# Attention rows of a one-core transformer layer: order of score blocks, output tail and products changed

## The chip, the core and the metric

The kernel runs on one core of one Trainium2 chip. A core has a matrix engine (TensorE, PE in the profile, with its weight loads as PEld), a vector engine (VectorE, DVE), a scalar engine for activation functions and copies (ScalarE, ACT), a general engine (GpSimd, POOL), and a queue engine that here only issues DMAs (SyncE, SP). Each engine works through its own instructions in order, and engines wait for each other through semaphores. Matrix results go to PSUM, which this stage divides into eight banks of 512 fp32 numbers in each of 128 partitions. The metric is the device time of one execution in microseconds (us).

## The reference

One layer of a hybrid backbone for two groups of tokens: 256 context tokens (the prompt) and 2048 latent tokens. Around the part that changes there are a projection, a Fourier mixing, an output projection and an MLP; they stay as they are. What changes is differential attention: for each of four heads there are two query/key halves, two softmaxes, and a difference of the two that is multiplied by the values.

```
s = jnp.einsum('bqhmd,bkhmd->bhmqk', qblk, k).astype(jnp.float32) * scale
p = jax.nn.softmax(s, axis=-1)
a = p[:, :, 0] - lam * p[:, :, 1]
return jnp.einsum('bhqk,bkhe->bqhe', a.astype(v.dtype), v)
```

Latent queries attend to 512 cached keys and to all 2048 latent keys, 2560 in all; prompt queries attend to the 256 prompt keys. Behind the attention each head's output is RMS-normalised.

## The kernel before

Before the attention stage, the kernel has written queries, keys and values to DRAM, most of them split into a high and a low part, so that fp32 products are made of three faster ones (`mm3`, L85 to L88).

**Groups and rows.** The stage runs over 4 heads and, in each, over 8 groups of 256 latent queries. A group is worked in four *rows*, one for each half j of its queries (128 each) and each softmax m: (j, m) = (0,0), (0,1), (1,0), (1,1). So there are 128 rows. In a row PE makes the five score blocks of the next row's softmax (`fill`, L918: 128 queries by 512 keys, two products each), VectorE takes the maximum of each block (`rowmax`, L923) and joins the five (`comb`, L926), and ScalarE makes the exponentials, with their sums, out of the five blocks that the row before had filled (`exp`, L942). When a half's two softmaxes are there, `combine` joins them: short VectorE work on the sums (L946, L947), then on GpSimd a scaling and an addition for the first 1024 keys and the same for the other 1536 (L964, L965).

**Products.** Six rows behind a group's start its products begin. The joined weights are transposed on PE in blocks of 2 x 128 keys for both halves (`tr`, L974, four transposes), ScalarE copies each transposed block out of PSUM (`ah`, L980), VectorE makes its low part (`al`, L985), and a row later PE multiplies by the values (`mul`). A group has ten such blocks, spread over four rows as 2, 3, 2 and 3. Two of the ten (key blocks 4 and 14, `FULL`) have no low part and are multiplied in plain fp32 (L998). The rows that transpose three blocks multiply two, and the rows that transpose two blocks multiply three, one of them in fp32.

**Output tail.** Five rows after its first transposes a group's output is finished. `o1` copies it out of PSUM (ScalarE, L1004), `o2` transposes it back (PE, L1008), `o3` copies that (VectorE, L1012), `o4` squares it with sums (ScalarE, L1018), `o5` makes the inverse root (VectorE L1021, then GpSimd L83), and `o6` scales it on GpSimd (L1027) and stores it with two DMAs (SyncE, L1028). All of that stands in the row in which the next group's first two blocks are multiplied; only the scaling spills into the row after it.

**Order.** The order of the work on each engine is written out by hand: `add(t, function, ...)` puts a step at a nominal time, in units `u` of a fifth of a row, and all steps are issued in the order of these times. The nominal times set only the order; the engines run when their waits are over. Prompt attention (`Prompt`) is put into a few rows of each head in the same way.

**PSUM.** Five banks (tag "S") hold score blocks, two (tag "pt") transposed blocks, one (tag "po") a group's output. With five score blocks a row and five banks, a block can be filled once the same block of the row before has been read by its exponential. A group allocates its own tile in the output bank with its first product:

```
if self.po is None:
    self.po = pS.tile([P, 512], F32, tag="po", name=f"po{self.nm}")
```

The first 256 columns take the sum of the products, the other 256 the transposed output.

Of the kernel before, what the change touches and what calls it, by code (L numbers as in the profile page):

```python
# [10 lines left out]
F32 = mybir.dt.float32  # L11
# [7 lines left out]
P = 128  # L19
# [21 lines left out]
def body(tc, a, out):  # L41
    nc = tc.nc
    ctx = ExitStack()
    with ctx:
# [40 lines left out]
        def mm3(ps, lh, ll, rh, rl, first, last):  # L85
            nc.tensor.matmul(ps, lh, rh, start=first, stop=False)  # L86
            nc.tensor.matmul(ps, lh, rl, start=False, stop=False)  # L87
            nc.tensor.matmul(ps, ll, rh, start=False, stop=last)  # L88
# [555 lines left out]
        with ExitStack() as c2:  # L644
# [106 lines left out]
            with tc.manual_schedule():  # L751
# [30 lines left out]
                A = [None] * 4  # L782
# [58 lines left out]
        with ExitStack() as c3_:  # L841
# [5 lines left out]
            ap = c3_.enter_context(tc.tile_pool(name="a_p", bufs=5, reuse_waits="tile"))  # L847
            kp = c3_.enter_context(tc.tile_pool(name="a_kp", bufs=1, reuse_waits="tile"))
            pS = c3_.enter_context(tc.tile_pool(name="a_ps", bufs=1, space=PSUM, reuse_waits="tile"))
            PCUT = 1024  # L850

            class Head:
# [28 lines left out]
            class Group:  # L881
                def __init__(self, hd, g):
                    self.hd, self.g, self.nm = hd, g, f"{hd.nm}_{g}"
                    self.S, self.mx, self.sm, self.p0, self.p1, self.tot = {}, {}, {}, {}, {}, {}
                    self.pt, self.A = {}, {}
                    self.po = None
                    self.nmul = 0
                    self.edge = 20 * g - 1 if hd.h == hd.s == 0 and g < 2 else None
                    self.last = hd.h == H - 1 and g == NS // 256 - 1

                    self.vcomb = 5 if self.last else 5 if hd.h == hd.s == g == 0 else 0
# [95 lines left out]

                def mul(self, kb):
                    if self.po is None:
                        self.po = pS.tile([P, 512], F32, tag="po", name=f"po{self.nm}")  # L990
                    A = self.A.pop(kb)
                    for t in range(2):
                        c = slice(t * 256, t * 256 + 256)
                        first = self.nmul == 0
                        self.nmul += 1
                        last = self.nmul == self.hd.nkt
                        if len(A) == 1:
                            nc.tensor.matmul(self.po[:, 0:256], self.hd.vf[kb][:, t, :], A[0][:, c], start=first, stop=last)  # L998
                        else:
                            mm3(self.po[:, 0:256], self.hd.V[:, kb + t, 0, :], self.hd.V[:, kb + t, 1, :], A[0][:, c], A[1][:, c], first, last)  # L1000

                def o1(self):
                    self.oT = at.tile([P, 256], F32, tag="oT", name=f"oT{self.nm}")
# [81 lines left out]
            def add(t, fn, *args):  # L1085
                ev.append((t, len(ev), fn, args))

            T = TSTEP
            u = T / 5.0
# [11 lines left out]
            for h in range(H):  # L1101
# [15 lines left out]
                for g in range(hd.ng):  # L1117
                    gr = Group(hd, g)
                    add(base - 2 * T + 0.6 * u if base else -3.03 * T, gr.qload)
                    for st in range(4):  # L1120
                        j, m = divmod(st, 2)
                        t0 = base + st * T
                        for b in range(hd.nbk):
                            add(t0 - T + (0.76 + 0.66 * b) * u, gr.fill, j, m, b)
                            add(t0 - T + (1.26 + 0.66 * b) * u, gr.rowmax, j, m, b)
                            add(t0 + 0.66 * b * u, gr.exp, j, m, b)
                        add(t0 - 0.45 * u, gr.comb, j, m)
                        if m:
                            add(t0 + 5.9 * u, gr.combine, j)
                    kbs = list(range(0, hd.nkt, 2))  # L1130
                    for q in range(4):
                        w = base + (AVS + q) * T
                        if q % 2 == 0:
                            order = [kbs.pop(0) for _ in range(2)]
                            tr_t, ah_t, al_t = [0.9, 2.2], [3.3, 3.8], [4.6, 5.2]
                        else:
                            order = [kbs.pop(0) for _ in range(3)]
                            tr_t, ah_t, al_t = [0.9, 2.2, 3.86], [3.3, 3.8, 4.4], [None, 4.6, 5.2]
                        for n, kb in enumerate(order):
                            add(w + tr_t[n] * u, gr.tr, kb)  # L1140
                            add(w + ah_t[n] * u, gr.ah, kb)
                            if al_t[n]:
                                add(w + al_t[n] * u, gr.al, kb)
                            add(w + T + (3.9 + 0.01 * n) * u, gr.mul, kb)
                    w = base + (AVS + 5) * T + 1.0 * u
                    for t, fn in ((0, gr.o1), (0.4, gr.o2), (0.75, gr.o3), (2.32, gr.o4), (3.557, gr.o5), (4.0, gr.o6)):
                        if gr.last and t > 2:
                            LASTO.append(fn)
                        else:
                            add(w + t * u, fn)  # L1150
                    base += 4 * T
# [754 lines left out]
```

## Time and profile before

| | |
|---|---|
| Median of 3 runs | 2971.24 us (2971.06 to 2977.52) |
| Profiled execution | 2976.96 us, span 2975.1 us |
| Instructions | 43755 |
| PE, PEld busy | 2910.2, 2518.0 us |
| DVE, ACT, POOL busy | 2016.3, 1568.3, 1023.9 us |
| Score products (L918), first to last | 571.3 to 1295.9 us of the span |
| Mean granted TensorE clock | 0.993 |

The span runs from the first to the last instruction of the profiled execution. "Busy" adds up the time in which an engine has an instruction running; PE's is an upper bound of its work, since matrix products are pipelined. In the timeline, a row gives the start and the length of a run of like instructions, the engine, the line of the kernel, the operation, output and inputs by the program's names, shapes and the count; brackets at the end give the idle time before it and what ended it. In the list of waits stand the engine, what it was about to write, whom it waited for, and the total, the count and the longest of these waits.

### The profile page before, as it was taken

The numbers are of one execution on the slowest core, as the hardware profiler recorded it, in microseconds if no ns is written. First come the engines' busy times: TensorE is split into PE (matmuls) and PEld (weight loads), VectorE is DVE, ScalarE is ACT, GpSimd is POOL, SyncE is SP. The second block draws the span as 40 slices with busy tenths as digits, with TensorE's granted clock in tenths as the row PEclk, the third lists the DMA queues.
The fourth block names the chain that finished last, engine by engine and source line by source line (L and its number), as shares of the span: only waits on it lengthen the run. The fifth ranks groups of instructions, "written<-read, shape, count | busy, mean of one in ns | idle before, by whom it ended". The sixth has DMA issues, their size and how long they took to land.

```text
span 2975.1 us, 43755 instructions
## 1 busy us (share of the span) xinstructions
PE 2910.2 (98%) x15417; PEld 2518.0 (85%) x15417; DVE 2016.3 (68%) x3379; ACT 1568.3 (53%) x3540; POOL 1023.9 (34%) x839
## 2 busy tenths in 40 slices
PE   8999999989999999999999999999999999999999
PEld 4888887768888888888889999999999888888887
DVE  6666775678888888875458778777776344344554
ACT  4333322678888888864346556556555322232221
POOL 1111112169898989952222333333332000000000
PEclk9999999989999999999999999999999999999999
DMA  7777878512131211215686677676666454445563
GB/s 274 202 195 198 232 197 250 195 52 84 35 110 37 91 53 34 95 50 157 202 252 213 217 240 225 220 237 214 222 199 229 145 170 163 138 145 173 195 216 107
DMA packets 394414, 495.58 MB, mean 167 GB/s; under 512 B 26403, under 2 KB 307056, under 8 KB 391122
## 3 DMA queue, kind: packets, MB, share of 16 engines
q1 hardware_dynamic: 386560, 477.63, 50.5%
q0 software_dynamic: 2992, 7.28, 0.8%
q10 hardware_dynamic: 4642, 7.88, 0.8%
q8 instruction: 122, 2.00, 0.3%
q14 instruction: 98, 0.80, 0.1%
HBM read 315.20 MB, written 179.57 MB: 166 GB/s over the span
## 4 chain that ended last, share of the span: by engine, by line
PE 84%; ACT 8%; DVE 4%; DMA 2%; issue 1%; POOL 0%; SPq 0%; ACTq 0%; DVEq 0%; POOLq 0%
PE Ss L918 8%; PE ps L86 8%; PE ps L87 8%; PE ps L88 8%; PE pj L86 4%; PE pj L88 4%; PE pj L87 4%; PE pts L974 4%; ACT P1s L942 3%; PE po L88 2%; PE po L86 2%; PE po L87 2%; PE pA L1532 2%; PE pA L1534 2%; PE pA L1533 2%; PE pC L1534 2%
## 5 line engine op out<-in xcount | busy, mean ns | idle before, releaser
L923 DVE TENSOR_REDUCE mxs<-Ss 128x1 f32<-128x512 f32 x640 | 419.4, 687 | 86.8 <-PE Ss L918 77.9
L1227 DVE TENSOR_TENSOR sl<-sr,sh 128x768 fp32r<-128x768 f32 x168 | 161.8, 964 | 339.8 <-ACT sh L1226 339.3
L965 POOL TENSOR_TENSOR P0s<-P0s,P1s 128x1024 f32<-128x1024 f32 x124 | 365.7, 2949 | 10.4
L1226 ACT CAST sh<-sr 128x768 fp32r<-128x768 f32 x168 | 140.2, 835 | 424.9 <-PE ps L87 424.9
L942 ACT ACTIVATE P1s<-Ss,mxs 128x512 f32<-128x512 f32 x320 | 217.2, 694 | 69.3 <-DVE mxs L926 69.3
L1574 POOL TENSOR_TENSOR gs<-g,g 128x384 f32<-128x384 f32 x48 | 70.3, 1464 | 483.7 <-ACT g L1544 376.7
L86 PE MATMUL pj<-wh,hh 128*128 128x512 f32 x576 | 229.8, 399 | 0.7 <-ACT fo L374 0.7
L87 PE MATMUL ps<-tlT,sh 128*128 128x512 f32 x585 | 229.3, 392 | 0.0
L86 PE MATMUL ps<-thT,sh 128*128 128x512 f32 x585 | 229.2, 392 | 0.0
L87 PE MATMUL pj<-wl,hh 128*128 128x512 f32 x576 | 227.7, 395 | 0.7 <-DVE wl L496 0.7
L88 PE MATMUL ps<-thT,sl 128*128 128x512 f32 x585 | 227.7, 389 | 0.0
L88 PE MATMUL pj<-wh,hl 128*128 128x512 f32 x576 | 226.7, 394 | 0.0
L942 ACT ACTIVATE P0s<-Ss,mxs 128x512 f32<-128x512 f32 x320 | 215.8, 696 | 7.8 <-DVE mxs L926 7.7
L918 PE MATMUL Ss<-KS1s,Qs 128*128 128x512 f32 x640 | 199.9, 426 | 13.6 <-ACT P0s L942 11.1
L918 PE MATMUL Ss<-KS0s,Qs 128*128 128x512 f32 x640 | 198.7, 423 | 10.5 <-ACT P1s L942 9.4
L974 PEld LDWEIGHTS pts<-ident,P0s 128*128 128x128 f32 x1280 | 158.0, 141 | 51.7 <-ACT ahs L980 5.7
L974 PE MATMUL pts<-ident,P0s 128*128 128x128 f32 x1280 | 193.0, 274 | 6.3 <-DVE alp L1071 4.1
L1543 ACT ACTIVATE g<-uz 128x384 f32<-128x384 f32 x144 | 75.9, 527 | 207.1 <-DVE uz L1566 180.6
L964 POOL TENSOR_SCALAR P1s<-P1s,tots 128x1024 f32<-128x1024 f32 x124 | 166.7, 1344 | 5.6
L985 DVE TENSOR_TENSOR als<-pts,ahs 128x512 fp32r<-128x512 f32 x256 | 163.9, 681 | 5.3 <-ACT ahs L980 5.3
L86 PE MATMUL ps<-ophT,sh 128*128 128x512 f32 x423 | 165.9, 392 | 1.1 <-DVE uz L1566 1.1
L88 PE MATMUL ps<-ophT,sl 128*128 128x512 f32 x423 | 165.7, 392 | 0.0
(613 smaller groups left out, 8216.1 us busy)
## 6 DMA issues: line engine op xcount, KB each, us to landing
sr<-sd SPq DMA_DIRECT2D x84, 768.0 KB, 4.4
a<-in_w SPq DMA_DIRECT2D x184, 256.0 KB, 3.8
sd<-gs SPq DMA_DIRECT2D x192, 192.0 KB, 1.9
sd<-g SPq DMA_DIRECT2D x144, 192.0 KB, 4.1
wm<-in_w_mod SPq DMA_DIRECT2D x32, 512.0 KB, 5.3
Qs<-qd SPq DMA_DIRECT2D x32, 512.0 KB, 3.7
b<-in_w SPq DMA_DIRECT2D x64, 256.0 KB, 5.2
b<-tsum SPq DMA_DIRECT2D x64, 256.0 KB, 4.6
```

Of the source, the lines that this page charges most:

```text
L86: nc.tensor.matmul(ps, lh, rh, start=first, stop=False)
L87: nc.tensor.matmul(ps, lh, rl, start=False, stop=False)
L88: nc.tensor.matmul(ps, ll, rh, start=False, stop=last)
L918: nc.tensor.matmul(S[:, :w], self.Q[:, x, m, j * P:j * P + P], self.hd.KS[m][:, b * 512:b * 512 + w], start=(x == 0), stop=(x == 1))
L923: nc.vector.tensor_reduce(self.mx[j][:, m, b:b + 1], self.S[j, m, b], axis=AX.X, op=ALU.max)
L942: nc.scalar.activation(dst, S, AF.Exp, bias=self.mx[j][:, m, 6:7], accum_out=self.sm[j][:, m, b:b + 1])
L964: nc.gpsimd.tensor_scalar(p, p, tot[:, 3:4], 0.0, op0=ALU.mult, op1=ALU.add)
L965: nc.gpsimd.tensor_add(d, d, p)
L974: nc.tensor.transpose(pt[:, c:c + P], self.p0[j][:, (kb + t) * P:(kb + t + 1) * P], ident)
L985: nc.vector.tensor_sub(t, self.pt[kb], f32(self.A[kb][0]))
L1226: nc.scalar.copy(hi, src)
L1227: nc.vector.tensor_sub(lo, src, f32(hi))
```

## The change

Five things in the attention stage, all in the order or the placing of work:

- The first transposed block of a row moves from behind score block 0 to behind score block 1, and the second from behind score block 2 to behind score block 3. The third stays behind score block 4.
- One PSUM tile `PO` serves all groups' output, instead of a tile for each group in the same bank.
- `o2` moves behind score block 1 of its row, and `o3` from between the first maxima of that row to behind its joined maximum and the subtractions, ahead of the next row's first maximum.
- `o4`, `o5` and `o6` move on by about a row: the squares go behind the next row's block copies, the inverse root and the scaling follow later in that row and the one after. The very last group keeps its own place for these three, and `o3` of it stays early.
- For key block 14, half of the first of its two fp32 products (the 128 queries of the first half) is taken a row earlier by `mul_part`; `mul` then does the other half of it, and the second product whole.

```diff
+            PO = pS.tile([P, 512], F32, tag="po", name="po")
...
-                    self.po = None
+                    self.po, self.half = None, []
...
-                        self.po = pS.tile([P, 512], F32, tag="po", name=f"po{self.nm}")
+                        self.po = PO
...
-                            nc.tensor.matmul(self.po[:, 0:256], self.hd.vf[kb][:, t, :], A[0][:, c], start=first, stop=last)
+                            x = P if kb in self.half and not t else 0
+                            nc.tensor.matmul(self.po[:, x:256], self.hd.vf[kb][:, t, :], A[0][:, t * 256 + x:t * 256 + 256], start=first, stop=last)
...
+                def mul_part(self, kb):
+
+                    self.half.append(kb)
+                    nc.tensor.matmul(self.po[:, 0:P], self.hd.vf[kb][:, 0, :], self.A[kb][0][:, 0:P], start=False, stop=False)
...
-                            tr_t, ah_t, al_t = [0.9, 2.2], [3.3, 3.8], [4.6, 5.2]
+                            tr_t, ah_t, al_t = [1.5, 2.8], [3.3, 3.8], [4.6, 5.2]
...
-                            tr_t, ah_t, al_t = [0.9, 2.2, 3.86], [3.3, 3.8, 4.4], [None, 4.6, 5.2]
+                            tr_t, ah_t, al_t = [1.5, 2.8, 3.86], [3.3, 3.8, 4.4], [None, 4.6, 5.2]
...
+                            if q == 3 and not n:
+                                add(w + 3.95 * u, gr.mul_part, kb)
...
-                    for t, fn in ((0, gr.o1), (0.4, gr.o2), (0.75, gr.o3), (2.32, gr.o4), (3.557, gr.o5), (4.0, gr.o6)):
-                        if gr.last and t > 2:
+                    for t, fn in ((0, gr.o1), (0.75, gr.o2), (0.95 if gr.last else 4.25, gr.o3), (8.5, gr.o4), (9.2, gr.o5), (9.6, gr.o6)):
+                        if gr.last and t > 5:
```

## The prediction

> **What bounds the kernel now.** I read the page first, then the stretches of time, the waits, and the timeline of one undisturbed group in the attention stage. All times are in microseconds.
>
> ```profile
> span 2975.1 us, 43755 instructions
> ...
> PE 2910.2 (98%) x15417; PEld 2518.0 (85%) x15417; DVE 2016.3 (68%) x3379; ACT 1568.3 (53%) x3540; POOL 1023.9 (34%) x839
> ```
>
> ```profile
> 650.00:1300.00 650.00, 635.90 (x4021) 538.51 (x4019) 564.11 (x1110) 573.41 (x1623) 582.79 (x469) 1.00 0.19 66
> ```
>
> The page's second line: TensorE works 98% of the span. The columns of the window are the length, then the busy time of PE, PEld, DVE, ACT and POOL, the granted clock, and DMA. In the 650 us that hold nearly the whole attention stage PE is busy 635.90, so PE's idle time there is 14.1; but each start after a wait also costs PE more than its idle time, as the rows below show. The four other columns are all at 83 to 90%: nothing has much room.
>
> ```profile
> DVE mxs L923 <- PE Ss L918: 77.9, 219, 2.4
> ...
> ACT P1s L942 <- DVE mxs L926: 69.3, 64, 5.2
> ...
> PEld Ss L918 <- ACT P0s L942: 31.9, 76, 2.5
> ```
>
> The three waits form a ring: maxima wait for scores, exponentials (exp) for the joined maximum, scores for an exp to empty their bank (five banks, five blocks a row). The rows of one group, on PE:
>
> ```profile
> 929.44 0.72 PE L918 MATMUL Ss<-KS1s,Qs 128*128 128x512 f32 x2
> ...
> 934.99 0.62 PE L918 MATMUL Ss<-KS0s,Qs 128*128 128x512 f32 x2
> ...
> 938.43 0.60 PE L974 MATMUL pts<-ident,P0s 128*128 128x128 f32 x4
> ...
> 940.68 0.73 PE L918 MATMUL Ss<-KS1s,Qs 128*128 128x512 f32 x2 [0.28 <-ACT P0s L942]
> ...
> 941.25 0.60 PE L974 MATMUL pts<-ident,P0s 128*128 128x128 f32 x4
> ...
> 943.98 1.02 PE L998 MATMUL pos<-ahs,vf4s 128*128 128x256 f32 x4
> ...
> 946.26 0.62 PE L918 MATMUL Ss<-KS0s,Qs 128*128 128x512 f32 x2
> ...
> 946.72 0.60 PE L974 MATMUL pts<-ident,P0s 128*128 128x128 f32 x4
> ...
> 949.45 0.60 PE L974 MATMUL pts<-ident,P0s 128*128 128x128 f32 x4
> ...
> 949.80 0.36 PE L86 MATMUL pos<-ahs,Vs 128*128 128x256 f32 x1
> ...
> 950.95 0.28 PE L86 MATMUL pos<-ahs,Vs 128*128 128x256 f32 x1
> ...
> 951.53 0.50 PE L918 MATMUL Ss<-KS1s,Qs 128*128 128x512 f32 x1
> ```
>
> A group of 256 queries takes four rows of work, each starting with score block 0 (L918): 929.44, 934.99, 940.68, 946.26, and the next group at 951.53. I call them R14 (ends with the fp32 products of block 14), RO (holds the old group's output tail), R4 (fp32 products of block 4) and RB. Lengths: 5.55, 5.69, 5.58, 5.27, together 22.09; 32 groups make 707 of the span. A score block costs 0.46 after products (946.26 to 946.72) and 0.57 when it had to wait (940.68 to 941.25). Four transposes take 0.35 (949.45 to 949.80); 946.72 to 949.45 is two such sets and two pairs of score blocks, so a pair takes 1.01, 0.505 for one in flow. RB's twelve products come in threes, 0.38 apart (949.80 to 950.95); the last three end at about 951.30, and PE then waits 0.23.
>
> ```profile
> 934.05 0.69 ACT L942 ACTIVATE P1s<-Ss,mxs 128x512 f32<-128x512 f32 x1 [1.01 <-DVE mxs L926]
> ...
> 938.11 0.36 ACT L1018 ACTIVATE osqs<-os 128x128 f32<-128x128 f32 x1
> ...
> 938.90 1.05 ACT L980 CAST ahs<-pts 128x512 fp32r<-128x512 f32 x2
> ...
> 939.84 0.70 ACT L942 ACTIVATE P0s<-Ss,mxs 128x512 f32<-128x512 f32 x1
> ...
> 945.29 0.69 ACT L942 ACTIVATE P1s<-Ss,mxs 128x512 f32<-128x512 f32 x1 [1.01 <-DVE mxs L926]
> ...
> 950.14 0.59 ACT L980 CAST ahs<-pts 128x512 fp32r<-128x512 f32 x1 [0.43 <-PE pts L974]
> ...
> 950.70 0.69 ACT L942 ACTIVATE P0s<-Ss,mxs 128x512 f32<-128x512 f32 x1
> ...
> 951.38 0.68 ACT L942 ACTIVATE P0s<-Ss,mxs 128x512 f32<-128x512 f32 x1
> ```
>
> ```profile
> 931.11 2.65 DVE L923 TENSOR_REDUCE mxs<-Ss 128x1 f32<-128x512 f32 x4 [0.21 <-PE Ss L918]
> ...
> 933.79 0.16 DVE L926 TENSOR_REDUCE mxs<-mxs 128x1 f32<-128x5 f32 x1
> ...
> 936.45 0.42 DVE L1012 COPY os<-pos 128x256 f32<-128x256 f32 x1
> ...
> 939.49 0.16 DVE L926 TENSOR_REDUCE mxs<-mxs 128x1 f32<-128x5 f32 x1
> ...
> 939.64 1.28 DVE L985 TENSOR_TENSOR als<-pts,ahs 128x512 fp32r<-128x512 f32 x2
> ...
> 946.92 0.69 DVE L923 TENSOR_REDUCE mxs<-Ss 128x1 f32<-128x512 f32 x1 [0.53 <-PE Ss L918]
> ...
> 950.51 0.16 DVE L926 TENSOR_REDUCE mxs<-mxs 128x1 f32<-128x5 f32 x1
> ```
>
> RO and RB end by the same ring: third transposed block, its copy (L980), exp 0, next score block. In RB: 949.45, 950.14, 950.70, 951.53, that is 0.69, 0.56 and 0.83. The maximum (950.51) comes 0.19 before the exp and binds here, for elsewhere the copy is followed by an exp after 0.48:
>
> ```profile
> 836.92 0.59 ACT L980 CAST ahs<-pts 128x512 fp32r<-128x512 f32 x1 [0.35 <-PE pts L974]
> ...
> 837.40 0.69 ACT L942 ACTIVATE P0s<-Ss,mxs 128x512 f32<-128x512 f32 x1
> ```
>
> In RO it is ScalarE that is late: it works without a break from 934.05 to 939.84, the two squares taking 0.79 of that (938.11 to 938.90). R14 and R4 end by PE: ScalarE waits 1.01 there before its first exp (945.29).
>
> **The change, part by part.** Each price is for one group.
>
> Score blocks 0 and 1 in a row. The fill behind a fill that waited must wait too, since exps are 0.68 apart (950.70, 951.38). The first rows of the stage show the pair without transposes between:
>
> ```profile
> 592.02 0.30 PEld L918 LDWEIGHTS Ss<-KS1s,Qs 128*128 128x128 f32 x2 [0.87 <-ACT P0s L942]
> ...
> 592.69 0.30 PEld L918 LDWEIGHTS Ss<-KS1s,Qs 128*128 128x128 f32 x2 [0.37 <-ACT P0s L942]
> ```
>
> Fill 0 starts 0.83 after its exp (950.70 to 951.53), fill 1 another 0.67 after fill 0. So in R14 and R4 three fills and one set of transposes take 0.67 + 0.57 + 0.35 + 0.505 = 2.10 instead of 0.57 + 0.35 + 1.01 = 1.93: +0.17 each, +0.34. What it saves is VectorE's gap between the first and the second maximum (0.21 at 931.11). In R14 and R4 PE ends the row, so that is worth nothing; in RB exp 0 then goes by the copy, 950.14 + 0.48 = 950.62 instead of 950.70: −0.08. The third transposed block stands behind five fills and two sets as before, so it is not earlier. Bounds: 0 if the fill never waits, +0.34 as shown; I take +0.34 because the first rows show this very pair.
>
> The Trainium skill, "TensorE: Matmul & The Clock Gate", Part 2, says that PE's queue pulls weight loads ahead of running matmuls; the rows agree where nothing waits (0.46), and the 0.57 is what a held weight load costs. By that rule with no hold the step would be free, which is the lower bound above.
>
> Output copy and norm later. The copy (936.45, 0.42 in the maxima's chain) and the squares leave RO. Without the squares ScalarE is ready at 939.05; without the copy the maximum allows 939.49 + 0.19 − 0.42 = 939.26; so the third transposed block binds: 938.43 + 0.69 + 0.48 = 939.60 instead of 939.84, −0.24. The squares go to R4 before its first exp, where ScalarE waits 1.01 and needs 0.79: 0; were that cover gone, 0.79. The copy goes behind the two subtractions (from 939.64, 1.28 long), ahead of R4's first maximum. R4's fifth maximum could start 0.77 + 4 × 0.665 = 3.43 after the row's start, but fill 4 lets it start only at 3.67 (below): 0.24 of cover, and VectorE's wait before the first maximum beside it. So 0; at most 0.42 − 0.24 = 0.18. The norm on GpSimd moves from before one combine to before the next one, where GpSimd has this gap:
>
> ```profile
> 952.25 0.34 POOL L948 TENSOR_SCALAR tots<-tots,nlam 128x1 f32<-128x1 f32 x1 [1.42 <-ACT P0s L942]
> ```
>
> Its power and two scalings fit there nearly or wholly; a combine that ends some tenths later is read by transposes that come more than a row behind it: 0. The two output stores per group, unchanged in number, leave the SyncE queue about a row later; only the next stage reads them, and no load of this stage waits for them: 0, at most some tenths at the very end.
>
> One PSUM tile. The next group's first product no longer waits for the copy of the old output. Nothing waits there now, so 0. The copy now shares a bank with products that are written meanwhile. The built order shows two new waits: the copy for PE, and R4's first fp32 product for the copy. RO's products end at about 940.25, and VectorE comes to the copy after its subtractions, at 940.92: 0.
>
> Products evened. Half of one fp32 product goes from R14 to RB. R4's end (943.98 to 946.26, 2.28) less RB's (949.80 to 951.30, 1.50) leaves 0.78 for two fp32 products; a quarter is 0.20. R14: −0.20. RB has PE's 0.23 of waiting for it: 0; without that cover +0.20, and a change of operand type may add a tenth, which the trace does not show for this place.
>
> What is late next. After R14, score block 1 of RO must wait for exp 1. In R14 fill 4 ends 3.30 (940.68 to 943.98) + 0.17 = 3.47 after the row's start; then 0.20 to its maximum (946.72 to 946.92), 0.665 for it (2.65/4), 0.29 to exp 0 (the joined maximum, 933.79 to 934.05, and 0.03), 0.68 to exp 1, 0.83 to the fill: 6.14 in all. PE is there at 5.55 + 0.17 − 0.20 + 0.46 = 5.98. So it waits 0.16 and pays 0.06 for the restart: +0.22. The shortening of R14 is given back here. After R4 PE arrives at 6.21: no wait.
>
> Sum for a group: 0.34 − 0.08 − 0.24 − 0.20 + 0.22 = +0.04; 32 groups, +1.3.
>
> Context tokens. In each head some rows also hold the prompt's work. Its subtraction blocks a transposed block once a head:
>
> ```profile
> 846.62 0.68 DVE L1071 TENSOR_TENSOR alp<-ptp,ahp 128x512 fp32r<-128x512 f32 x1
> ```
>
> ```profile
> 847.45 0.63 PE L974 MATMUL pts<-ident,P0s 128*128 128x128 f32 x4 [1.02 <-DVE alp L1071]
> ```
>
> PE waits 1.02 there. The subtraction no longer stands behind the output copy: −0.4. After these transposes only one score block is left before the third transposed block instead of two: −0.5. In three more rows of a head the prompt's exps delay a score block behind which the transposes (0.35) now stand, or squares and copy leave the row as in RO (−0.24 each): I set them against each other, bounds −0.5 and +0.35. Four heads: −3.6 (bounds −6 and 0).
>
> Total: +1.3 − 3.6 = −2.3. The profiled execution took 2976.96 (span 2975.1), 5.7 above the median of 2971.24, so the forecast is 2974.7 on its own scale and 2969 as a median.
>
> **The rivals.** *Faster, by the wait that doesn't come.* If fill 1 isn't held (exp 0 so early that fill 0 doesn't wait, and the banks come free ahead of it), the +0.34 and +0.22 fall: −0.52 a group, −17, with the prompt −20: 2951. For it: PE would then be the only bound, and copy and squares do leave the ring. Against it: the ring through the third transposed block is not shortened, and the first rows' 0.67. It decides if fill 1 starts under 0.57 after fill 0.
>
> *Slower, by the same ring in all rows.* If the way from fill 4 over maximum and exp 1 to the next fill 1 is 0.2 longer than I reckon, the wait grows in RO by 0.2 and reaches RB as well (6.34 against 6.21, and 0.06 for the restart): 0.39 a group, 12.5 over the forecast, 2981. It decides from 6.21 on (the arrival of PE after R4), 0.07 above my figure, so it is not far.
>
> *Slower, by the shared bank.* If the copy ends up waiting for products that run into the following row, VectorE stands with the maxima behind it. From 0.67 of delay (940.92 against 940.25) each tenth costs up to 3.2; 0.4 beyond it is 13 over the forecast, 2982. The Trainium skill, "PSUM — Partial Sum Buffer", section "PSUM bank collisions raise a hardware error", tells to guard by bank and not by address, even where columns differ; by that rule this wait must be there. The row of 939.64 gives it its spare time.
>
> *Nothing happens*: every part is covered, 2971; it falls within the forecast.
>
> **How the numbers follow.** A measurement of this kernel can tell about 0.3%, 9 us. The forecast with "nothing happens" 0.50 (own range 2961 to 2979), faster 0.28, slower by the ring 0.17, by the bank 0.05. Few runs of the forecast's case leave the 9 us, as many on either side. So faster 0.29, same 0.49, slower 0.22. The range for 8 in 10 reaches to both: 2949 to 2982.
>
> **What would show it.** In the changed kernel's timeline: fill 1 in R14 and R4 starting 0.67 after fill 0 with a wait for ScalarE (wrong if under 0.57); RO about 5.6 to 5.7 long, exp 0 there directly behind the third copy; ScalarE's wait before R4's first exp down from 1.01 to about 0.2; R14 5.5; the 1.02 wait for the prompt's subtraction gone; the group 22.0 to 22.2. I am wrong if the group is under 21.8 or over 22.4.

## The result, and the profile after

The changed kernel takes 2977.91 us (median of 22 runs, 2974.75 to 2983.79), the kernel before 2973.69 beside it (22 runs, 2969.93 to 2977.52). The ratio is 1.0017, with a 95% interval of 1.0011 to 1.0024: slower by 4.2 us between the medians and by 5 us by the ratio, within the 0.3% that I had called "same", but on the other side of the forecast of 2.3 us faster.

The page of the changed kernel, its second line of busy times, and the stretch that holds nearly all of the attention stage (columns as before):

```profile
span 2975.5 us, 43868 instructions
...
PE 2914.6 (98%) x15481; PEld 2512.7 (84%) x15481; DVE 2025.9 (68%) x3379; ACT 1580.1 (53%) x3540; POOL 1022.5 (34%) x839
```

```profile
650.00:1300.00 650.00, 640.40 (x4052) 533.89 (x4051) 569.94 (x1101) 582.14 (x1614) 579.36 (x468) 1.00 0.19 67
```

PE is busy for 640.40 of the 650, 4.5 more than before. The change adds no product (it splits one in two); a row of PE also grows when a score block is held and starts again: below, two score blocks (x4) stand with 1.40 where they are held and with 1.13 where they are not. The list of waits of the changed kernel shows the holding:

```profile
DVE mxs L925 <- PE Ss L920: 69.9, 191, 1.9
...
PEld Ss L920 <- ACT P1s L944: 42.2, 88, 5.7
PEld Ss L920 <- ACT P0s L944: 39.2, 106, 2.5
...
ACT P1s L944 <- DVE mxs L928: 33.4, 35, 5.2
...
PE Ss L920 <- DMA Qs<-qd: 0.9, 3, 0.4
```

and in the kernel before, beside the three lines that the prediction shows:

```profile
PEld Ss L918 <- ACT P1s L942: 24.2, 50, 5.7
```

ScalarE's wait for the joined maximum is halved (33.4, from 69.3) and the maxima wait less for PE. But PE's weight loads for score blocks, which waited 31.9 in 76 places for the exponentials of the first softmax and 24.2 in 50 for those of the second, now wait 39.2 in 106 and 42.2 in 88. The last line, a wait of score blocks for the loads of queries, is not in the list of the kernel before.

An undisturbed group on PE, with the rows named as in the prediction; R14 starts at 1085.52, RO at 1091.04, R4 at 1096.80, RB at 1102.58, and the next group at 1107.77:

```profile
1085.52 1.40 PE L920 MATMUL Ss<-KS1s,Qs 128*128 128x512 f32 x4
1086.76 0.60 PE L976 MATMUL pts<-ident,P0s 128*128 128x128 f32 x4
...
1091.04 1.38 PE L920 MATMUL Ss<-KS0s,Qs 128*128 128x512 f32 x4
1092.26 0.60 PE L976 MATMUL pts<-ident,P0s 128*128 128x128 f32 x4
...
1092.83 1.21 PE L920 MATMUL Ss<-KS0s,Qs 128*128 128x512 f32 x4
1093.88 0.60 PE L976 MATMUL pts<-ident,P0s 128*128 128x128 f32 x4
1094.23 0.71 PE L920 MATMUL Ss<-KS0s,Qs 128*128 128x512 f32 x2
1094.79 0.60 PE L976 MATMUL pts<-ident,P0s 128*128 128x128 f32 x4
...
1096.80 1.40 PE L920 MATMUL Ss<-KS1s,Qs 128*128 128x512 f32 x4
1098.03 0.60 PE L976 MATMUL pts<-ident,P0s 128*128 128x128 f32 x4
...
1102.58 1.13 PE L920 MATMUL Ss<-KS0s,Qs 128*128 128x512 f32 x4
1103.55 0.60 PE L976 MATMUL pts<-ident,P0s 128*128 128x128 f32 x4
...
1107.77 1.41 PE L920 MATMUL Ss<-KS1s,Qs 128*128 128x512 f32 x4
```

Rows of 5.52, 5.76, 5.78 and 5.19, together 22.25; before 22.09, forecast 22.13. The first two score blocks take 1.24 in R14 (1085.52 to 1086.76), 1.22 in RO, 1.23 in R4, and 0.97 in RB, the only row where nothing holds them. The score block that now stands alone between two sets of transposes takes 0.56 (1094.23 to 1094.79), where a pair takes 1.01.

On ScalarE the steps of the tail are where they were expected: in RO exp 0 follows the third copy by 0.48, and in R4 the squares stand right ahead of exp 0, whose wait of 1.01 is gone. The joined maximum of RO, on VectorE, comes 0.25 ahead of exp 0.

```profile
1095.48 0.59 ACT L982 CAST ahs<-pts 128x512 fp32r<-128x512 f32 x1 [0.32 <-PE pts L976]
1095.96 0.69 ACT L944 ACTIVATE P0s<-Ss,mxs 128x512 f32<-128x512 f32 x1
...
1101.01 0.31 ACT L1026 ACTIVATE osqs<-os 128x128 f32<-128x128 f32 x1
1101.48 0.69 ACT L944 ACTIVATE P1s<-Ss,mxs 128x512 f32<-128x512 f32 x1
```

```profile
1095.71 0.16 DVE L928 TENSOR_REDUCE mxs<-mxs 128x1 f32<-128x5 f32 x1
```

**A wait that no part of the prediction has.** In some groups R14 is 5.9 to 6.2 long. One such row runs from 902.80 to 909.01. SyncE's queue, GpSimd, ScalarE and PE there:

```profile
903.45 0.80 SPq L1036 DMA_DIRECT2D att<-os  x2
904.34 1.71 SPq L897 DMA_DIRECT2D Qs<-qd  x1
```

```profile
898.77 3.52 POOL L967 TENSOR_TENSOR P0s<-P0s,P1s 128x1536 f32<-128x1536 f32 x1
902.23 0.72 POOL L83 TENSOR_TENSOR osss<-osss,mhalf 128x2 f32<-128x2 f32 x1
903.05 0.72 POOL L1035 TENSOR_SCALAR os<-os,osss 128x128 f32<-128x128 f32 x2
```

```profile
907.45 0.70 ACT L944 ACTIVATE P1s<-Ss,mxs 128x512 f32<-128x512 f32 x1 [0.86 <-DVE mxs L928]
```

```profile
909.01 1.16 PE L920 MATMUL Ss<-KS0s,Qs 128*128 128x512 f32 x4 [0.55 <-ACT P1s L944]
```

The queries of the next group (L897) are loaded by the same queue as the output stores (L1036), and behind them. The stores wait for the scaling (L1035), the scaling for the root (L83), and this now stands behind GpSimd's long addition, which ends at 902.3. So the load is issued at 904.34, and RO's first score block, which reads these queries, would be free to start 0.83 after its exp (907.45), at 908.28, but starts at 909.01. The bracket names ScalarE; that exp had long begun, so I put the wait down to the load; the run with the loads ahead, below, bears it out. Before, the same load left the queue 15 us ahead of its use:

```profile
941.01 0.80 SPq L1028 DMA_DIRECT2D att<-os  x2
941.90 0.38 SPq L895 DMA_DIRECT2D Qs<-qd  x1
```

That load is for RO at 957.11. In the changed kernel it leaves about 4 us ahead of its use in every undisturbed group. What a load takes stands in the page's list of DMA issues of the changed kernel (count, size of each, median time from issue to landing):

```profile
Qs<-qd SPq DMA_DIRECT2D x32, 512.0 KB, 3.5
```

When a load, or a store ahead of it, is slower than usual, PE stands. In the profiled run five groups pay: 22.62, 22.66, 22.56, 22.70 and 22.38 (R14 at 697.04, 741.88, 880.24, 902.80, 1063.14) against 22.25, together 1.7.

### The profile page after: what moved, and what is told of

It is laid out like the page before. It is cut to its first block, busy times and chain, and to the rows that moved or that the text cites. A ratio compares the mean times of both kernels' runs of the same rounds, so it can differ in the third digit from the quotient of the medians.

```text
span 2975.5 us, 43868 instructions
## 1 busy us (share of the span) xinstructions
PE 2914.6 (98%) x15481; PEld 2512.7 (84%) x15481; DVE 2025.9 (68%) x3379; ACT 1580.1 (53%) x3540; POOL 1022.5 (34%) x839
## 4 chain that ended last, share of the span: by engine, by line
PE 90%; DVE 3%; ACT 2%; DMA 2%; issue 1%; POOL 1%; SPq 0%; ACTq 0%; DVEq 0%; POOLq 0%
PE Ss L920 10%; PE ps L86 8%; PE ps L87 8%; PE ps L88 8%; PE pj L86 4%; PE pj L88 4%; PE pj L87 4%; PE pts L976 4%; PE po L88 4%; PE po L86 4%; PE po L87 4%; PE pA L1542 2%; PE pA L1543 2%; PE pB L1542 2%; PE pA L1544 2%; PE pC L1544 2%
## 5 line engine op out<-in xcount | busy, mean ns | idle before, releaser
L944 ACT ACTIVATE P1s<-Ss,mxs 128x512 f32<-128x512 f32 x320 | 217.3, 694 | 35.6 <-DVE mxs L928 33.4
L920 PE MATMUL Ss<-KS1s,Qs 128*128 128x512 f32 x640 | 210.9, 434 | 4.8 <-ACT P0s L944 4.0
L982 ACT CAST ahs<-pts 128x512 fp32r<-128x512 f32 x256 | 151.3, 593 | 47.9 <-PE pts L976 39.7
```

The costliest lines, as they stand in the source:

```text
L920: nc.tensor.matmul(S[:, :w], self.Q[:, x, m, j * P:j * P + P], self.hd.KS[m][:, b * 512:b * 512 + w], start=(x == 0), stop=(x == 1))
L944: nc.scalar.activation(dst, S, AF.Exp, bias=self.mx[j][:, m, 6:7], accum_out=self.sm[j][:, m, b:b + 1])
L982: nc.scalar.copy(t, self.pt[kb])
```

## The experiments

The theory after the result: the new order of score blocks costs more than the tail and the products bring, and the late query loads come on top. The first rival: the order costs nothing, and the later tail, the shared tile or the split product is at fault. Row lengths, here and in the table, are differences of the starts of score block 0 on PE in an undisturbed group; the ratio is to the kernel before, timed beside it on the same chip.

| kernel | R14 | RO | R4 | RB | group | median | before | ratio, 95% interval |
|---|---|---|---|---|---|---|---|---|
| before (929.44) | 5.55 | 5.69 | 5.58 | 5.27 | 22.09 | | | |
| after (1085.52) | 5.52 | 5.76 | 5.78 | 5.19 | 22.25 | 2977.91 | 2973.69 | 1.0017, 1.0011 to 1.0024 |
| order undone (1108.55) | 5.45 | 5.64 | 5.58 | 5.29 | 21.96 | 2975.15 | 2974.49 | 1.0002, 0.9993 to 1.0011 |
| queries ahead (1087.04) | 5.57 | 5.70 | 5.80 | 5.20 | 22.27 | 2976.94 | 2974.49 | 1.0008, 1.0000 to 1.0017 |
| order alone (931.10) | 5.76 | 5.66 | 5.76 | 5.27 | 22.45 | 2984.31 | 2974.49 | 1.0032, 1.0019 to 1.0044 |
| tail alone (951.40) | 5.54 | 5.52 | 5.54 | 5.29 | 21.89 | 2980.55 | 2974.49 | 1.0019, 1.0011 to 1.0028 |
| products alone (1107.12) | 5.45 | 5.81 | 5.58 | 5.28 | 22.12 | 2973.10 | 2974.23 | 0.9997, 0.9989 to 1.0006 |
| tail, queries ahead (1105.79) | 5.57 | 5.51 | 5.54 | 5.30 | 21.92 | 2970.81 | 2973.96 | 0.9991, 0.9982 to 1.0000 |
| and products (1105.49) | 5.45 | 5.63 | 5.56 | 5.28 | 21.92 | 2970.80 | 2973.96 | 0.9986, 0.9977 to 0.9995 |
| second transposes late (1106.98) | 5.51 | 5.74 | 5.72 | 5.21 | 22.18 | 2974.91 | 2973.96 | 1.0005, 0.9996 to 1.0013 |
| new order in RB only (1150.17) | 5.42 | 5.62 | 5.56 | 5.39 | 21.99 | 2972.89 | 2973.96 | 0.9995, 0.9986 to 1.0003 |
| root given its place (1103.40) | 5.44 | 5.62 | 5.56 | 5.28 | 21.90 | 2969.73 | 2974.23 | 0.9985, 0.9976 to 0.9994 |

**The order undone.** Against the kernel after:

```diff
-                            tr_t, ah_t, al_t = [1.5, 2.8], [3.3, 3.8], [4.6, 5.2]
+                            tr_t, ah_t, al_t = [0.9, 2.2], [3.3, 3.8], [4.6, 5.2]
...
-                            tr_t, ah_t, al_t = [1.5, 2.8, 3.86], [3.3, 3.8, 4.4], [None, 4.6, 5.2]
+                            tr_t, ah_t, al_t = [0.9, 2.2, 3.86], [3.3, 3.8, 4.4], [None, 4.6, 5.2]
```

> The changed kernel with the transposes back in their old places (behind score blocks 0, 2 and 4); tail, one tile and evened products stay. Theory A (the new order of the score blocks costs: a held second fill of 0.17 in R14 and R4, a wait of about 0.25 in RO, and some 0.04 a row for a score block left alone between transposes; the other parts gain, but some of their gain is given back at the next ring): the group falls from 22.26 to about 21.9 to 22.0, some 10 us under the changed kernel in the whole, less 2 us that the prompt rows lose, so about 3 to 5 us under the kernel before. Rival B (the later tail, the shared tile or the split product cost, the order does not): it stays with the changed kernel, 3 to 5 us over the kernel before.

The undisturbed group falls to 21.96, as the theory has it, 0.29 under the kernel after. But the time comes out level with the kernel before, not 3 to 5 under it. The rest is in R14: with shorter rows the query loads have less time still (3.65 in the group at 1108.55, where the kernel after has 3.94 at 1085.52), and R14 reaches 6.69 (1063.56 to 1070.25).

**The query loads ahead of the stores.** Against the kernel after:

```diff
-                    add(base - 2 * T + 0.6 * u if base else -3.03 * T, gr.qload)
+                    add(base - 3 * T + 0.5 * u if base else -3.03 * T, gr.qload)
```

> The changed kernel with each query load issued ahead of the old group's output stores on SyncE. Theory A (in some groups the load stands behind stores that wait for GpSimd, and RO's first score block waits for it): R14 rows of 5.8 to 6.2 become 5.54, and about 8 to 10 groups give back 0.35 each, 3 us; the rest stays, so 1 to 2 us over the kernel before. Rival (the long row is made good by the short row that follows it): same time as the changed kernel, 4 to 5 us over the kernel before.

All undisturbed groups are 22.21 to 22.32 long and no R14 row without prompt work is over 5.6: the cause of the long rows is the place in the queue. It accounts for some 1.5 us (112 rows take 638.58 against 640.05), half of what I expected, since I had counted eight to ten late groups and five paid. The two medians lie 1.0 apart, or 1.8 if each is taken against the kernel before that was timed beside it (2.45 over it, and 4.22).

**The order alone**, in the kernel before:

```diff
-                            tr_t, ah_t, al_t = [0.9, 2.2], [3.3, 3.8], [4.6, 5.2]
+                            tr_t, ah_t, al_t = [1.5, 2.8], [3.3, 3.8], [4.6, 5.2]
...
-                            tr_t, ah_t, al_t = [0.9, 2.2, 3.86], [3.3, 3.8, 4.4], [None, 4.6, 5.2]
+                            tr_t, ah_t, al_t = [1.5, 2.8, 3.86], [3.3, 3.8, 4.4], [None, 4.6, 5.2]
```

> The kernel before with only the transposes moved behind score blocks 1, 3 and 4. Theory A: held fill 0.17 twice, lone block 0.04 four times, 0.08 gained in RB: 0.43 a group, 14 us, less some 2 us in prompt rows: 12 us slower than before (10 to 17). Rival B (order costs nothing): within 2 us of the kernel before.

9.8 us slower, just under the range of 10 to 17: the group is 22.45, 0.36 longer, 0.21 of it in R14 and 0.18 in R4; in the three groups of a head that hold prompt work only 0.5 is lost (24.80 + 23.85 + 23.05 from 998.46 on against 24.17 + 24.24 + 22.79 from 814.07 on in the kernel before). The rival is out. RB, where I had forecast 0.08 less, is 5.24 to 5.29.

**The tail alone.** The kernel after without the new order and without the evened products:

```diff
-                            tr_t, ah_t, al_t = [1.5, 2.8], [3.3, 3.8], [4.6, 5.2]
+                            tr_t, ah_t, al_t = [0.9, 2.2], [3.3, 3.8], [4.6, 5.2]
...
-                            tr_t, ah_t, al_t = [1.5, 2.8, 3.86], [3.3, 3.8, 4.4], [None, 4.6, 5.2]
+                            tr_t, ah_t, al_t = [0.9, 2.2, 3.86], [3.3, 3.8, 4.4], [None, 4.6, 5.2]
...
-                            if q == 3 and not n:
-                                add(w + 3.95 * u, gr.mul_part, kb)
```

> The kernel before with only the tail moved (output copy behind the joined maximum, squares, root, scaling and stores a row later, one tile for all groups' output). Theory A: RO falls from 5.69 to about 5.45, of which R4 or RB give back up to half; 4 to 8 us gained, up to 3 of them lost again to query loads that come late: 2 to 6 us under the kernel before. Rival B (the later tail or the shared tile costs): 3 to 5 us over it.

Against the theory's sign: 6 us slower. The reason isn't the rival's. The undisturbed group is short, 21.89, but most groups are not undisturbed. The worst, from 1111.44 to 1118.21, on SyncE's queue and PE:

```profile
1112.38 1.81 SPq L1036 DMA_DIRECT2D att<-os  x2
1114.28 0.38 SPq L897 DMA_DIRECT2D Qs<-qd  x1
```

```profile
1118.21 0.70 PE L920 MATMUL Ss<-KS0s,Qs 128*128 128x512 f32 x2 [1.05 <-ACT oTs L1012]
```

The two stores took 1.81 to issue instead of 0.80, the load behind them left at 1114.28, and R14 is 6.77 long. Fourteen groups are together 9 us over 21.91, nearly all of it in R14. I had allowed 3 for it.

**The tail with the query loads ahead**, the kernel of the tail alone with this edit:

```diff
-                    add(base - 2 * T + 0.6 * u if base else -3.03 * T, gr.qload)
+                    add(base - 3 * T + 0.5 * u if base else -3.03 * T, gr.qload)
```

> The kernel with only the tail moved, and each query load issued ahead of the old group's output stores. Theory (the later tail gains 0.19 in an undisturbed group, 22.09 to 21.90, and some 0.65 a head in rows with prompt work; the query load that stands behind the later stores costs it all, up to 1.2 in one row): all groups without prompt work at 21.9, no R14 row over 5.6, and 0.19 x 20 + 0.65 x 4, some 6 us under the kernel before. Rival (the long R14 rows have another cause, such as GpSimd): they stay, and the time stays 3 to 6 us over the kernel before.

9 us faster than without that edit (3.2 under its own runs of the kernel before, against 6.1 over them), and faster than the kernel before by a little (its interval ends at 1.0000); all R14 rows without prompt work are 5.53 to 5.59. So the tail itself gains, and the price of its place was paid by the loads. The 6 us that I expected came only by half. Some 1.4 of what is missing lies in the first head after the start, where five RB rows are 5.44 to 5.48 long, and one with prompt work 6.45 instead of 5.92 (see the last experiment).

RO shows the tail's gain, 0.17, and what limits it. ScalarE and VectorE, row start at 1111.36:

```profile
1115.48 0.59 ACT L982 CAST ahs<-pts 128x512 fp32r<-128x512 f32 x1 [0.39 <-PE pts L976]
1116.04 0.69 ACT L944 ACTIVATE P0s<-Ss,mxs 128x512 f32<-128x512 f32 x1
```

```profile
1112.92 1.39 DVE L925 TENSOR_REDUCE mxs<-Ss 128x1 f32<-128x512 f32 x2 [0.21 <-PE Ss L920]
1114.52 1.29 DVE L925 TENSOR_REDUCE mxs<-Ss 128x1 f32<-128x512 f32 x2 [0.21 <-PE Ss L920]
1115.84 0.16 DVE L928 TENSOR_REDUCE mxs<-mxs 128x1 f32<-128x5 f32 x1
```

Exp 0 comes 0.56 behind the copy and 0.20 behind the joined maximum: the maximum binds. It stands 4.48 after the row's start, with the output copy in its chain 4.50 (939.49 less 934.99). Taking 0.42 of work out of VectorE only made it wait for PE twice.

**Tail, products and query loads ahead**, the kernel after with these edits:

```diff
-                    add(base - 2 * T + 0.6 * u if base else -3.03 * T, gr.qload)
+                    add(base - 3 * T + 0.5 * u if base else -3.03 * T, gr.qload)
...
-                            tr_t, ah_t, al_t = [1.5, 2.8], [3.3, 3.8], [4.6, 5.2]
+                            tr_t, ah_t, al_t = [0.9, 2.2], [3.3, 3.8], [4.6, 5.2]
...
-                            tr_t, ah_t, al_t = [1.5, 2.8, 3.86], [3.3, 3.8, 4.4], [None, 4.6, 5.2]
+                            tr_t, ah_t, al_t = [0.9, 2.2, 3.86], [3.3, 3.8, 4.4], [None, 4.6, 5.2]
```

> The same with the evened products as well: the changed kernel with the transposes in their old places and the query loads ahead of the stores. Theory (the evened product takes 0.1 from R14 and gives 0.1 back in RO): group 21.9 as without it, 6 to 7 us under the kernel before, within 1.5 us of the one without evened products. Rival (the evened products gain by themselves, as the 5 us between the two kernels with late query loads would say): some 5 us faster than without them, 11 under the kernel before.

Within 0.01 us of the kernel without the products: they give nothing of their own in an undisturbed group. R14 is 5.45 instead of 5.57, and RO 5.63 instead of 5.51. In the rows with prompt work the traces show some 0.35 less a head (three groups from 991.37 on take 70.29, against 70.64 from 991.33 on without the products), 1.4 us over four heads, which the medians don't show. (The 5.4 us between the two kernels with late loads came from the loads, then, not from the products.) This version is faster than both the kernel before and the kernel after.

**The products alone**, the kernel before with `mul_part`, its counterpart in `mul`, and:

```diff
+                            if q == 3 and not n:
+                                add(w + 3.95 * u, gr.mul_part, kb)
```

> The kernel before with only the evened products. Theory (R14 is shortened by 0.1, and RO, which ends by the ring over exp 0, gives it back): R14 5.45, RO 5.79, group 22.09 as before; about 0.35 a head may stay in rows with prompt work, so 0 to 2 us under the kernel before. Rival (the product taken out of R14 stays gained): R14 5.45 or less with RO still 5.69, group 21.9 to 22.0, 3 to 6 us under the kernel before.

The same picture without the tail: R14 5.45, RO 5.81, group 22.12, and a time that can't be told from the kernel before.

**Only the second transposes late.** The order of the kernel after split in two, with the query loads ahead:

```diff
-                            tr_t, ah_t, al_t = [1.5, 2.8], [3.3, 3.8], [4.6, 5.2]
+                            tr_t, ah_t, al_t = [0.9, 2.8], [3.3, 3.8], [4.6, 5.2]
...
-                            tr_t, ah_t, al_t = [1.5, 2.8, 3.86], [3.3, 3.8, 4.4], [None, 4.6, 5.2]
+                            tr_t, ah_t, al_t = [0.9, 2.8, 3.86], [3.3, 3.8, 4.4], [None, 4.6, 5.2]
```

> The changed kernel with the query loads ahead, the first transposes of a row behind score block 0 again, and the second still behind block 3, so that no second fill follows a held one at once, but block 4 still stands alone. Theory (holding and standing alone are two costs): the held fills (0.17 in R14 and R4) and RO's wait go, the lone block's 0.04 a row stays: group about 22.05 to 22.1, the time about 5 us under that of the changed kernel with query loads ahead, 2 to 4 under the kernel before. Rival (only the held fill costs): group 21.9, 6 to 7 under the kernel before. Rival (only the place of the second transposes costs): group 22.2.

The theory missed: the group is 22.18, close to the 22.2 of the second rival, so the held second fill can't be the whole price. R4 on PE:

```profile
1118.23 0.73 PE L920 MATMUL Ss<-KS1s,Qs 128*128 128x512 f32 x2
...
1119.14 1.81 PE L920 MATMUL Ss<-KS1s,Qs 128*128 128x512 f32 x6
1120.80 0.60 PE L976 MATMUL pts<-ident,P0s 128*128 128x128 f32 x4
1121.15 0.71 PE L920 MATMUL Ss<-KS1s,Qs 128*128 128x512 f32 x2
1121.70 1.02 PE L1001 MATMUL po<-ahs,vf4s 128*128 128x256 f32 x4
```

The three score blocks take 1.66 (1119.14 to 1120.80); in RB of the same kernel three take 1.52. Exps are 0.67 apart, so behind a fill 0 that waited, fill 3 can't start before 3 x 0.67 = 2.0 after it. PE would be there at 0.91 + 1.01 = 1.92, is held 0.08 and pays the restart. The trace has fill 3 at 2.01 in this row, 0.85 after the start of the exp that empties its bank, where fill 3 of RB starts 0.90 after its own and isn't held. In the old order PE reaches fill 3 only at 2.28 (0.57 + 0.35 + 1.01 + 0.35), since two sets of transposes lie before it. So it is the pace of the exps that any early group of fills runs into, the second or the fourth. The lone block's 0.05 is in this row too (1121.15 to 1121.70).

**The new order in RB alone**, where the pair wasn't held (in the kernel with products, tail and query loads ahead):

```diff
-                            tr_t, ah_t, al_t = [0.9, 2.2, 3.86], [3.3, 3.8, 4.4], [None, 4.6, 5.2]
+                            tr_t, ah_t, al_t = [1.5 if q == 3 else 0.9, 2.8 if q == 3 else 2.2, 3.86], [3.3, 3.8, 4.4], [None, 4.6, 5.2]
```

> The later tail, the evened products, the query loads ahead, and the new order of score blocks and transposes in RB rows alone, where the pair did not wait (0.97 for two blocks). Theory: RB 5.27 to 5.20, the other rows as without it, so the group is 21.85 and the time some 2 us under that of the same kernel without it, 8 to 9 under the kernel before. Rival (what RB gains is given back in R14, which then finds exp 0 no earlier): same as without it, 6 to 7 under the kernel before.

RB grows from 5.28 to 5.32 to 5.42 instead of falling to 5.20, and the time is 1.1 under the kernel before, where the same kernel without it is 3.2 under; neither the theory nor the rival had that. With R4 5.56 long instead of 5.78, PE comes to RB earlier, and its pair is held there too: it takes 1.10 and more instead of 0.97. So RB's 5.19 in the kernel after hangs on the longer R4. That isn't all of it: with the order alone R4 is as long, and RB is 5.24 to 5.29.

**The root given its place.** In the kernel with tail, products and query loads ahead, VectorE's step of the root (`o5`) had the same nominal time as the second subtraction of its row, and rounding decided which came first:

```diff
-                    for t, fn in ((0, gr.o1), (0.75, gr.o2), (0.95 if gr.last else 4.25, gr.o3), (8.5, gr.o4), (9.2, gr.o5), (9.6, gr.o6)):
+                    for t, fn in ((0, gr.o1), (0.75, gr.o2), (0.95 if gr.last else 4.25, gr.o3), (8.5, gr.o4), (9.1, gr.o5), (9.6, gr.o6)):
```

> The kernel with later tail, evened products and query loads ahead, transposes in their old places, and VectorE's step of the root given a nominal time of its own (it shared one with the second subtraction of the row, so that in some groups it stood behind that, where it took 1.3 instead of 0.4 and the maxima came late). Theory: it takes 0.4 in all groups, the RB rows of 5.45 to 5.50 become 5.28 and the RB row with prompt work falls from 6.5 to about 5.9, 1.5 us in all: 4 to 5 us under the kernel before. Rival (the time depends on GpSimd and not on the order): RB rows and time as without it, 3 to 4 us under the kernel before.

The best of all, 4.5 us under the kernel before. Every RB row without prompt work is 5.26 to 5.29, the row of 6.5 is 5.87, and the step takes 0.34 to 0.44 throughout; without the edit it took 1.3 in the groups in which it came second. VectorE and GpSimd in one of those (kernel without this edit):

```profile
739.39 1.32 DVE L1029 SCALAR_TENSOR_TENSOR osss<-osss,s0es 128x2 f32<-128x2 f32 x1
740.63 1.28 DVE L925 TENSOR_REDUCE mxs<-Ss 128x1 f32<-128x512 f32 x2
```

```profile
739.15 1.55 POOL L966 TENSOR_SCALAR P1s<-P1s,tots 128x1536 f32<-128x1536 f32 x1
```

A step on 128x2 numbers ends at 740.71, with GpSimd's scaling (740.70), and the maxima stand behind it. In the kernel before it took 0.16:

```profile
939.57 0.16 DVE L1021 SCALAR_TENSOR_TENSOR osss<-osss,s0es 128x2 f32<-128x2 f32 x1
```

## Why the prediction was wrong, step by step

Two steps failed: the loads behind the moved stores, put at nothing, cost 1.5 us, and the score blocks cost 0.12 a group more than reckoned, 3.8 us in all. Row by row the forecast's terms make 5.52 for R14, 5.67 for RO, 5.75 for R4 and 5.19 for RB; measured are 5.52, 5.76, 5.78 and 5.19.

*"Score blocks 0 and 1 in a row": +0.34 in R14 and R4. Right in kind, short by 0.05 or so.* The pair takes 1.23 to 1.24 as reckoned (0.67 + 0.57). Missed was that regrouping 1 + 2 + 2 into 2 + 2 + 1 leaves a block alone, at 0.55 instead of 0.505; the term took three fills and one set of transposes and stopped there. Done alone the order costs 0.39 in these two rows. *The −0.08 in RB* came in the kernel after (5.19 to 5.23), but it isn't the order's own: alone the order leaves RB at 5.24 to 5.29, and in RB rows only it makes them longer.

*"What is late next": +0.22 in RO; measured about +0.32.* Score block 1 of RO is held by exp 1, as forecast. But the five score blocks of RO take 1.22 + 1.05 + 0.56 = 2.83 in the kernel after and 0.46 + 1.04 + 1.01 = 2.51 before (934.99 to 935.45, and the rows here; the third transposed block follows at 938.43). Half of the missing 0.1 is again the block left alone. So the third transposed block comes 3.75 after the row's start instead of 3.66 (3.44 + 0.22), and RO is 0.09 longer than forecast.

```profile
935.45 0.60 PE L974 MATMUL pts<-ident,P0s 128*128 128x128 f32 x4
...
936.02 1.20 PE L918 MATMUL Ss<-KS0s,Qs 128*128 128x512 f32 x4
937.06 0.60 PE L974 MATMUL pts<-ident,P0s 128*128 128x128 f32 x4
937.42 1.18 PE L918 MATMUL Ss<-KS0s,Qs 128*128 128x512 f32 x4
```

*"Output copy and norm later": −0.24 in RO; measured −0.17 with the old order.* There the step that failed is "without the copy the maximum allows 939.26", where I took the copy's full 0.42 out of the maxima's chain: it waits for PE instead. In the kernel after this step is as wrong but costs nothing, since the third copy binds, as forecast: exp 0 follows it by 0.48, and the joined maximum by 0.25, where it binds at 0.19. The squares were hidden in R4, as forecast.

*"Only the next stage reads them, and no load of this stage waits for them: 0."* This is the step that failed outright: a term put at nothing. It looked at who reads the stores and not at what stands behind them in SyncE's queue: the next query load, with 4 us of margin instead of 15. It cost 1.5 us in the changed kernel, some 4 with the order undone (0.7 over the kernel before against 3.2 under it with the loads ahead), and 9 with the tail alone.

*"Products evened": −0.20 in R14, and given back in RO.* With the old order they come to 0 in an undisturbed group, alone (22.12) and with the tail (21.92). The cause differs a little: R14 can't fall below 5.45 in the old order, because exp 0 stands 4.61 after its start (934.05 less 929.44) and the next fill 0.83 after that; the other 0.1 was never to be had there. With the new order R14 does fall, from 5.76 to the forecast 5.52; no run there parts the products from the tail.

*One tile: 0.* No wait for it shows in the rows of any kernel; it was not run by itself. *The prompt's rows: −0.9 a head, right.* The RO row in which PE had waited 1.02 falls from 6.8 to 5.9. In a head from 992.35 on the three groups with prompt work take 24.55 + 23.44 + 22.80 = 70.79, 0.41 less than the 71.20 before, where three undisturbed groups' 0.16 each would have made it 0.48 more; no wait for the prompt's subtraction is left. In the head from 809.07 on the step of the root took 0.3 of it back.

The account: an undisturbed group costs +0.16 instead of +0.04, which over 32 groups is 5.1 instead of 1.3; the prompt −3.6 as forecast, 0.3 less in one head; the loads +1.5 instead of 0. That makes +3.3, against a difference of the medians of 4.2. The parts run by themselves agree: 22.09, and 0.36 for the order, −0.17 for the tail and 0 for the products, make 22.28 for a group, and 22.25 to 22.27 are measured. The remaining 1 us I can't place. Outside the rows single profiles differ by more: the stage starts at 567.8 to 571.3 in the twelve profiled runs, and from the first score block of the last row to the end of the span pass 1682.3 to 1685.7, with no order by the change; so the spans of two profiles can't be set against each other here.

Of the rivals, "slower by the same ring in all rows" named the right resource, but PE's waits stayed in the rows where the forecast had them; the shared bank and the faster cases did not show. Of the signs, the group of 22.25 lies outside the 22.0 to 22.2 that were to show the forecast. The result lies in the range and in the likeliest case; its sign was lost to the score blocks and to the queue.

## What to carry to other kernels

A step that is moved takes its DMAs with it: ask for every store on an in-order queue what load stands next in that queue, how far ahead of its use it was, and how far ahead it will be. When a ring paces an engine (here one bank free every 0.67), work that fits between its steps is free and is best left there; putting two paced steps together only makes the second wait and start again. And gains in one row are gains only if the row after it doesn't end by the same ring: read the sum over the whole period, not the row.

## What the runs showed of the hardware

- A VectorE step with two inputs in SBUF waited for GpSimd's running instruction to end, however small it was: 1.32 instead of 0.16 for 128x2 numbers. The two ends agree within 0.01 us in all seven groups of that kernel in which the step took 1.27 to 1.34. The Trainium skill, "SBUF — State Buffer", section "SBUF: two separate sides", tells that such a VectorE operation and a GpSimd operation that reads SBUF lock each other out of a port pair for a whole instruction; the rows agree.
- The issue of the same two stores took 0.80 in most groups and 1.6 to 1.9 in some, that of a query load 0.38 or up to 1.8. Which groups meet the slow one, and why, the runs don't tell; where the stores were slow ahead of a late load, R14 was longest (6.77 with the tail alone and 6.69 with the order undone).
- A score block between two sets of transposes took 0.55, against 1.01 for two and 1.52 for three in a row: about 0.05 for standing alone. I have no reading for its cause.
